# First mixture matrix in 8 KB runs, and the turn of the inner values moved between the scatter or gather products

## The chip, the cores and the metric

One core of one Trainium2 chip runs the whole program. The time is device microseconds (us) of one execution; the number that counts is the median of several. The engines are PE (the matrix engine; its loads of stationary operands are listed as PEld), DVE, ACT, POOL and SP. In this kernel SP issues nearly all of the loads from memory, and the 16 DMA engines of the core move them.

## The reference, cut to what matters

Two layers over 256 tokens of 2048 features, in float32. Each layer has a mixer (retention and convolution in the first, sparse attention in the second), a norm, and then a mixture of 16 experts of which every token takes two:

```
for e in range(N_EXPERTS):
    a, b = jnp.split(xt @ w_gu[e], 2, axis=-1)
    y = y + gate[:, e:e + 1] * ((jax.nn.silu(a) * b) @ w_down[e])
```

`w_gu[e]` is 2048 x 1024 (8 MB) and is here called the first matrix, `w_down[e]` is 512 x 2048 (4 MB), the second. A layer reads 16 x 12 MB for its mixture, whatever the routing is.

## The kernel before, in words

The tokens of an expert are gathered into 64 slots, so that the products of a mixture are small beside the weights that they read. Experts go in pairs `i` = 0..7 with members `j` = 0, 1. The order of the work is written out by hand in `moe` (L1020 to L1048); each engine works through its own list in that order.

- Weights come in chunks of 1 MB, one DMA each, through the list that `plan` makes (L115 to L123). A chunk fills one of 22 pages of 8 KB a partition. `pump` (L145) issues the next chunk from SP as soon as a page is free and fewer than `ringmax` chunks (16 in most of a mixture) are held. A chunk of the first matrix (L118) has 256 rows as 2 blocks of 128: row p of each block lies in partition p, so each partition takes two separate runs of 4 KB. A chunk of the second matrix (L121) is 128 rows of 2048 values: one run of 8 KB a partition, the megabyte as a whole contiguous in memory. The four chunks of the last expert's second matrix are columns, in runs of 2 KB.
- `gather(i, c)` (L865) makes 512 features of the slots of a pair: the tokens `h` are the stationary operand, 128 columns at a time, a one-hot matrix is the moving one. Each product is two loads and two products in the trace. ACT or DVE copies the result to `X[i]`.
- `gu(i, j)` (L894) takes 8 chunks and multiplies 64 slots by them, with two products side by side in the two column halves of the array; then ACT (silu, L907) and DVE (product, L908) make the inner values `sl`.
- `turn` (L911) transposes `sl` on PE (L914) and ACT copies it to `gT` (L916); `down(i, j, gT)` (L931) multiplies `gT` by four chunks of the second matrix, and ACT and DVE (L928, L929) make the rows `Y`.
- `scatter(i)` (L964) puts the rows of a pair at their tokens: 8 blocks of 4 products (L951), each followed by a DVE addition (L959 for the first pair, L961 later).
- For a pair the order is: `gu(i, 0)`, `scatter(i - 1)`, `turn`, `down(i, 0)`, `gather(i + 1, 0 and 1)`, `gu(i, 1)`, `gather(i + 1, 2 and 3)`, `gates(i + 1)` (L877, transposes and products with 2 columns), `turn`, `down(i, 1)`. The PSUM tiles of gather, scatter and turn share 4 banks (L172).
- After the last `gu` come its `turn` (L1044), a branch for experts with too many tokens (L1061), and `last_down` (L972), which uses the last four chunks.

Of the kernel before, what the change touches and what calls it, by code (L numbers as in the profile page):

```python
# [19 lines left out]
P = 128  # L20
# [11 lines left out]
# columns of the constant arrays  # L32
# [48 lines left out]
class Trunk:  # L81
# [9 lines left out]
    # ---------------------------------------------------------------- pages of 8 KB a partition  # L91
# [5 lines left out]
    def drop(self, n=1):  # L97
        """n pages have seen their last use"""
        self.free += n
        self.pump()  # L100

    # ---------------------------------------------------------------- weights
    def plan(self):
        a = self.a
        ch = []

        def dense(w, cols, order):
            for g, kc in order:
                c0, n = cols[g]
                if n == 512:  # L110
                    ch.append((w[kc * 512:(kc + 1) * 512, c0:c0 + n].rearrange("(c p) n -> p c n", p=P), [P, 4, n]))
                else:
                    ch.append((w[:, c0:c0 + n].rearrange("(c p) n -> p c n", p=P), [P, 16, n]))

        def moe(layer):  # L115
            for e in range(NE):
                for k in range(8):
                    ch.append((a["moe_w_gu"][layer, e, k * 256:(k + 1) * 256, :].rearrange("(c p) n -> p c n", p=P), [P, 2, 1024]))  # L118
                for k in range(4):
                    if e < NE - 1:  # L120
                        ch.append((a["moe_w_down"][layer, e, k * P:(k + 1) * P, :].rearrange("(c p) n -> p c n", p=P), [P, 1, 2048]))  # L121
                    else:
                        ch.append((a["moe_w_down"][layer, e, :, k * 512:(k + 1) * 512].rearrange("(c p) n -> p c n", p=P), [P, 4, 512]))  # L123

        # of each projection (column group, part of the rows), in the order of their use
        std = lambda n: [(g, kc) for g in range(n) for kc in range(4)]
        cols = [(c * 512, 512) for c in range(4)]
        self.eorder = [(g, kc) for g in range(4) for kc in (2, 3, 0, 1)]
        self.oorder = [(g, kc) for g in (0, 1) for kc in (0, 1, 2)] + [(0, 3), (1, 3)] + [(g, kc) for g in (2, 3) for kc in range(4)]
        self.ecols = [4096, 5120, 4608, 5632, 0, 512, 1024, 1536, 2048, 2560, 3072, 3584]  # L130
        dense(a["even_w_in"][0], [(c, 512) for c in self.ecols], std(12))
        dense(a["even_w_out"][0], cols, self.eorder)
        moe(0)
        self.ocols = [(3072, 512), (3584, 512), (4096, 80), (2048, 512), (2560, 512)] + [(c * 512, 512) for c in range(4)]
        dense(a["odd_w_in"][0], self.ocols, [(g, kc) for g, kc in std(9) if g != 2 or kc == 0])
        dense(a["odd_w_out"][0], cols, self.oorder)
        moe(1)
        self.chunks = ch
        self.next = 0
        self.got = {}  # L140
        self.use = 0
        self.ring = 0
        self.ringmax = 1
# [27 lines left out]
    # ---------------------------------------------------------------- helpers  # L171
# [34 lines left out]
    # ---------------------------------------------------------------- dense projections  # L206
    def units(self, groups, order=None):
        """the steps of projections: two blocks of rows each (four of a narrow group)"""
        us = []
        seen = {}  # L210
        for i, kc in order or [(i, kc) for i, g in enumerate(groups) for kc in range(4 if g.n == 512 else 1)]:
            g = groups[i]
            for s in range(2 if g.n == 512 else 4):
                n = seen[i] = seen.get(i, -1) + 1
                if g.n == 512:
                    us.append(dict(g=g, k=kc * 4 + s * 2, first=n == 0, last=n == 7, sub=s, nsub=2, w=2))
                else:
                    us.append(dict(g=g, k=s * 4, first=s == 0, last=s == 3, sub=s, nsub=4, w=4))
        return us
# [51 lines left out]
    def dense(self, us, between, hooks=None, budget=1.3, ahead=3, tail=5):  # L271
        hooks = hooks or {}
        n = 0
# [18 lines left out]
        # the end of the last group: one token tile, then the other  # L292
# [10 lines left out]
    # ---------------------------------------------------------------- start  # L303
    def setup(self):
# [20 lines left out]
        # x and the first weights in the pieces and the order of their use  # L325
# [26 lines left out]
    def warm(self, n):  # L352
        """products that nobody wants, to keep the clock of the tensor engine up while it waits"""
        ps = self.psum("warm").rearrange("p (a n) -> p a n", a=4)
        for _ in range(n):
            self.nc.tensor.matmul(ps, self.ones, self.ones[:, None, :].to_broadcast([P, 4, P]), start=True, stop=True)

    def table(self, func):
        """have the activation table of func loaded by the time it is wanted"""
        self.nc.scalar.activation(self.tiny, self.neghalf[:, 0:1], func)  # L360
# [40 lines left out]
    def halves(self, name):  # L401
        """the two parts of a transposed operand, each [128, 8, 256] for half of the rows"""
        return [self.page(f"{name}{i}", [P, 8, S], F32R) for i in range(2)]

    # ---------------------------------------------------------------- even layer
# [235 lines left out]
    def rope(self, out, ps, cos, sin, heads, half):  # L641
        """out, ps: [128, heads*2*half]; the halves of each head apart"""
# [26 lines left out]
    def moments(self, t):  # L669
        """1 / std and - mean / std of token tile t"""  # L670
# [6 lines left out]
    def norm(self, c):  # L677
        """columns of (acc - mean) / std, in place"""
# [8 lines left out]
    def normed(self, t):  # L687
        """token tile t of (acc - mean) / std, in place"""
# [10 lines left out]
    def norms(self, kp):  # L699
        """the columns that the turns up to kp + 1 need"""  # L700
# [3 lines left out]
    def turned(self, kp, out, gc, bc):  # L704
        """out = g * turned + b for the two blocks of kp"""
# [14 lines left out]
    # ---------------------------------------------------------------- mixture of experts  # L720
    def route(self, mp, pl):
        """slots, gates and counts: all [128 tokens, 2 tiles, 16 experts]"""
# [15 lines left out]
        # groups: the largest sum of two, the first of the largest ; experts: how many of the group go before each  # L738
# [44 lines left out]
    def onehot(self, i):  # L783
        """slot one-hots of the experts A, B of pair i, in the order A B A"""
# [8 lines left out]
    def moe_begin(self, layer):  # L793
        """what can be done when the first token tile is normed"""
# [8 lines left out]
    def turned_half(self, layer, t, c):  # L803
        """h = g z + b, 512 columns of token tile t turned"""
# [15 lines left out]
    def moe(self, layer, before_last=None):  # L820
# [14 lines left out]
        def back(t, c):  # L835
            """h as it lies in acc"""
# [28 lines left out]
        def gather(i, c):  # L865
            """features 4c to 4c + 3 of the tokens in the slots of pair i, a slot a column"""
            ps = self.psum("psg")
            for b in range(4):
                k = c * 4 + b
                for t in range(2):  # L870
                    nc.tensor.matmul(ps[:, b * P:(b + 1) * P], h[t][:, k * P:(k + 1) * P], self.PT[i][:, t, 0:P], start=t == 0, stop=t == 1)
# [5 lines left out]
        def gates(i):  # L877
            """one-hots with a slot a row, for the orders A B and B A, and the gates of the slots"""
# [15 lines left out]
        def gu(i, j):  # L894
            ps = self.bank("pgu")
            for c in range(8):
# [3 lines left out]
                wv = w.rearrange("p k (ab h f) -> p k ab h f", ab=2, h=2)  # L900
# [18 lines left out]
        # a product of slots with w_down: of each two blocks of 256 columns one lies in the upper rows, the other in the lower,  # L919
        # and the other way round for the second expert, so that in Y[i][:, o] both experts have rows for the same columns  # L920
        def weigh(i, j, half, po, c0):
            """the upper or lower rows of a product times the gates, in two exact parts"""
# [24 lines left out]
        def placed(i, t, c, ps, begun=False):  # L947
            """the rows of the slots at their tokens, 512 columns of tile t"""
# [15 lines left out]
        def scatter(i):  # L964
            if i == 0:
                self.acc = [self.page(f"z{t}") for t in range(2)]
            for t in range(2):
                for c in range(4):
                    spread(i, t, c)
            self.drop(2)  # L970

        def last_down(gT, early):  # L972
            """the last expert, 512 columns after the other up to the statistics of the norm"""
            begun = {}

            def begin(b, alloc):
                """what acc holds, so that the sum stands in PSUM"""
# [42 lines left out]
        for i in range(8):  # L1020
            if i == 7:
                self.ringmax = 8
            if 0 < i < 7:
                self.onehot(i + 1)
            sl = gu(i, 0)
            if i:
                scatter(i - 1)
# [4 lines left out]
            down(i, 0, turn(sl))  # L1032
# [4 lines left out]
            if i < 7:  # L1037
                gather(i + 1, 2)
                gather(i + 1, 3)
                gates(i + 1)  # L1040
                down(i, 1, turn(sl))
# [9 lines left out]
    def overflow(self, layer, rv, h, wide):  # L1051
        """tokens beyond the slots of an expert: every expert over all tokens, with the gates of those alone"""
# [37 lines left out]
    # ---------------------------------------------------------------- odd layer  # L1090
    def odd(self):
# [142 lines left out]
        def q_done(j):  # L1234
            def f(ac):
# [9 lines left out]
                def task():  # L1245
# [5 lines left out]
                    # one head after the other, a step apart  # L1251
# [86 lines left out]
    # ---------------------------------------------------------------- end  # L1338
# [54 lines left out]
```

## Time and profile before

| what | value |
|---|---|
| time, median of 3 runs (lowest to highest) | 1726.28 us (1724.84 to 1727.17) |
| span of the profiled execution | 1722.4 us (no time outside the span is listed for it; the median is 3.9 us longer) |
| PE busy | 1634.8 us, 95% of the span |
| DVE, ACT, POOL busy | 743.9, 500.6, 345.3 us |
| read from memory | 524.7 MB, 306 GB/s over the span |
| mixtures | products L904 from 407.4 to 850 us (first layer) and to 1675.8 us (second) |
| PE waits for chunks of the first matrix (L904) | 10.8 us over the span, at the ends of the mixtures |

The busy share of PE counts an instruction from its start to its modelled end, and neighbours overlap; so 95% says only that PE is seldom idle. For a single stretch it is better to take starts of instructions and to subtract. In the slice lines each of the 40 places stands for 43 us of the span.

### The profile page before, as it was taken

To read this page: it belongs to the slowest core of one execution; us is meant where nothing else is said; L and a number is where in the kernel's file an instruction comes from. 1 tells how busy PE (TensorE), PEld (TensorE's weight loads), DVE (VectorE), ACT (ScalarE), POOL (GpSimd) and SP (SyncE) were. 2 spreads that over 40 slices of the span, in tenths; PEclk is the share of its full clock that TensorE was granted. 3 is DMA by queue.
4 is the path that set the end of the run, shared out by engine and by line. 5 is a ranking of instruction groups with operands and counts; after the bars stand their busy time and mean duration, and the time that the engine had idled before them with its cause. 6 is when DMAs were issued, how large, how long until landed. Compare 5 with 4: busy or idle time off the path is not lost. (4 is left out here: it accounts for less than half of the span.)

```text
span 1722.4 us, 21361 instructions
## 1 busy us (share of the span) xinstructions
PE 1634.8 (95%) x8551; PEld 1031.0 (60%) x8551; DVE 743.9 (43%) x1348; ACT 500.6 (29%) x780; POOL 345.3 (20%) x218
## 2 busy tenths in 40 slices
PE   9999999999999999999789999999999999999974
PEld 7888887885454445443268788788644544444422
DVE  5799987533222222221264675654412322232125
ACT  5434345433111111111054535553311111111101
POOL 1446564430000000000024553434000000000010
PEclk9999999999999999999989999999999999999996
DMA  9655546859999999999954554366899999999992
GB/s 339 218 189 172 171 150 208 300 201 360 372 410 411 413 413 411 415 412 413 401 187 137 167 186 131 123 221 246 342 370 404 414 412 414 412 413 413 412 406 76
DMA packets 155628, 528.29 MB, mean 307 GB/s; under 512 B 10506, under 2 KB 10898, under 8 KB 140034
## 3 DMA queue, kind: packets, MB, share of 16 engines
q1 hardware_dynamic: 154898, 525.32, 80.2%
q8 instruction: 71, 1.16, 0.3%
q0 software_dynamic: 480, 1.46, 0.2%
q14 instruction: 35, 0.29, 0.0%
q10 hardware_dynamic: 144, 0.07, 0.0%
HBM read 524.71 MB, written 2.10 MB: 306 GB/s over the span
## 5 line engine op out<-in xcount | busy, mean ns | idle before, releaser
L904 PE MATMUL pgu<-w,X 128*64 128x512 f32 x2048 | 450.9, 594 | 11.0 <-DMA w<-in_moe_w_gu_dram 10.8
L236 POOL TENSOR_TENSOR sp<-w,sp 128x1024 fp32r<-128x1024 f32 (+1 forms) x108 | 273.0, 2535 | 402.5 <-ACT sp L233 377.2
L904 PEld LDWEIGHTS pgu<-w,X 128*64 128x64 f32 x2048 | 143.7, 137 | 300.2 <-issue 267.3
L233 ACT ACTIVATE sp<-w 128x1024 fp32r<-128x1024 f32 (+1 forms) x228 | 230.4, 1045 | 121.7 <-PE acc L267 64.1
L236 DVE TENSOR_TENSOR sp<-w,sp 128x1024 fp32r<-128x1024 f32 (+1 forms) x120 | 185.8, 1552 | 130.0 <-ACT sp L233 129.7
L939 PE MATMUL pdn<-w,gT 128*64 128x512 f32 x960 | 212.6, 596 | 16.1 <-ACT gT L916 16.1
L929 DVE SCALAR_TENSOR_TENSOR Yl<-pdn,gs,Yh 64x512 fp32r<-64x512 f32 (+1 forms) x136 | 97.6, 718 | 290.5 <-ACT Yh L928 276.7
L928 ACT ACTIVATE Yh<-pdn,gs 64x512 fp32r<-64x512 f32 (+1 forms) x136 | 89.4, 657 | 283.6 <-PE pdn L939 183.6
L908 DVE TENSOR_TENSOR sl<-sl,pgu 128x256 f32<-128x256 f32 x32 | 13.5, 421 | 354.2 <-ACT sl L907 354.2
L265 PE MATMUL acc<-sp,xhi 128*128 128x512 f32 x384 | 152.4, 397 | 0.0
L939 PEld LDWEIGHTS pdn<-w,gT 128*64 128x64 f32 x960 | 66.3, 137 | 143.1 <-issue 116.1
L266 PE MATMUL acc<-sp,xhi 128*128 128x512 f32 x384 | 149.8, 390 | 0.3 <-DVE sp L236 0.3
L267 PE MATMUL acc<-sp,xlo 128*128 128x512 f32 x384 | 149.9, 390 | 0.0
L791 POOL COPY pt<-pt 128x128 f32<-128x128 f32 x16 | 5.0, 314 | 714.1 <-DVE pt L790 714.1
L907 ACT ACTIVATE sl<-pgu 128x256 f32<-128x256 f32 x32 | 12.3, 384 | 387.1 <-PE pgu L904 377.0
L469 DVE SCALAR_TENSOR_TENSOR pcv<-up,cw,pcv 128x255 f32<-128x255 f32 (+14 forms) x240 | 113.2, 472 | 7.3
L265 PE MATMUL acc<-sp,hhi 128*128 128x512 f32 x256 | 106.1, 414 | 1.2 <-ACT hhi L1116 1.2
L267 PE MATMUL acc<-sp,hlo 128*128 128x512 f32 x256 | 101.1, 395 | 1.2 <-DVE hlo L1117 1.2
L266 PE MATMUL acc<-sp,hhi 128*128 128x512 f32 x256 | 100.6, 393 | 0.0
L266 PEld LDWEIGHTS acc<-sp,xhi 128*128 128x128 f32 x384 | 72.3, 188 | 15.3 <-DVE sp L236 1.0
L267 PEld LDWEIGHTS acc<-sp,xlo 128*128 128x128 f32 x384 | 72.1, 188 | 15.2
L265 PEld LDWEIGHTS acc<-sp,xhi 128*128 128x128 f32 x384 | 72.3, 188 | 14.8 <-ACT sp L233 0.4
(305 smaller groups left out, 2050.7 us busy)
## 6 DMA issues: line engine op xcount, KB each, us to landing
w<-in_moe_w_gu_dram SPq DMA_DIRECT2D x256, 1024.0 KB, 17.6
w<-in_moe_w_down_dram SPq DMA_DIRECT2D x128, 1024.0 KB, 18.4
w<-in_even_w_in_dram SPq DMA_DIRECT2D x46, 1024.0 KB, 5.3
w<-in_odd_w_in_dram SPq DMA_DIRECT2D x32, 1024.0 KB, 5.4
w<-in_even_w_out_dram SPq DMA_DIRECT2D x16, 1024.0 KB, 8.6
w<-in_odd_w_out_dram SPq DMA_DIRECT2D x16, 1024.0 KB, 5.5
acc<-in_x_dram SPq DMA_DIRECT2D x8, 256.0 KB, 8.3
w<-in_even_w_in_dram SPq DMA_DIRECT2D x4, 512.0 KB, 6.7
```

The source lines that it names most:

```text
L233: nc.scalar.activation(sp[:, 0], src, AF.Copy)
L236: eng.tensor_tensor(sp[:, 1], src, sp[:, 0].bitcast(F32), ALU.subtract)
L265: nc.tensor.matmul(ac, xh[:, x], wh, start=st, stop=False)
L266: nc.tensor.matmul(ac, xh[:, x], wl, start=False, stop=False)
L267: nc.tensor.matmul(ac, xl[:, x], wh, start=False, stop=en)
L469: nc.vector.scalar_tensor_tensor(y, up[:, c, 0:S - i], w, y, op0=ALU.mult, op1=ALU.add)
L904: nc.tensor.matmul(ps[h * 64:(h + 1) * 64, :], X[i][:, k, j * 64:(j + 1) * 64], wv[:, kk, :, h, :], start=k == 0, stop=k == KT - 1)
L907: nc.scalar.activation(sl, ps[:, 0:256], AF.Silu)
L908: V.tensor_tensor(sl, sl, ps[:, 256:512], ALU.mult)
L928: nc.scalar.activation(hi, po[r, :], AF.Copy, scale=g)
L929: V.scalar_tensor_tensor(lo, po[r, :], g, hi.bitcast(F32), op0=ALU.mult, op1=ALU.subtract)
L939: nc.tensor.matmul(po[b][half * 64:(half + 1) * 64, :], gT[:, c, h * 64:(h + 1) * 64], wv[:, half ^ j, 2 * b:2 * b + 2, :], start=kk == 0, ...
```

## The change

In `plan` a chunk of the first matrix is read with partition p holding the rows 2p and 2p + 1 of its 256, so each partition takes one run of 8 KB. The k-th block of 128 features of `X` therefore has to hold every second feature of 256; `gather` takes its stationary operand from `h` with a step of two values. `turn` stands after the first token tile of the scatter (j = 0) or between the third and fourth part of the gather (j = 1). For the first member of the first pair, and for the last member of the last pair, its place stays.

```
     def plan / moe(layer):
-        ch.append((a["moe_w_gu"][layer, e, k * 256:(k + 1) * 256, :].rearrange("(c p) n -> p c n", p=P), [P, 2, 1024]))
+        ch.append((a["moe_w_gu"][layer, e, k * 256:(k + 1) * 256, :].rearrange("(p c) n -> p (c n)", c=2), [P, 2048]))
...
     def gather(i, c):
-                k = c * 4 + b
-                for t in range(2):
-                    nc.tensor.matmul(ps[:, b * P:(b + 1) * P], h[t][:, k * P:(k + 1) * P], self.PT[i][:, t, 0:P], start=t == 0, stop=t == 1)
+                q, r = divmod(c * 4 + b, 2)
+                for t in range(2):
+                    f = h[t].rearrange("p (q j r) -> p q r j", q=8, r=2)[:, q, r, :]
+                    nc.tensor.matmul(ps[:, b * P:(b + 1) * P], f, self.PT[i][:, t, 0:P], start=t == 0, stop=t == 1)
...
     def gu(i, j):
-                wv = w.rearrange("p k (ab h f) -> p k ab h f", ab=2, h=2)
+                wv = w.rearrange("p (k ab h f) -> p k ab h f", k=2, ab=2, h=2)
...
-        def scatter(i):
-            if i == 0:
+        def scatter(i, t):
+            if i == 0 and t == 0:
                 self.acc = [self.page(f"z{t}") for t in range(2)]
-            for t in range(2):
-                for c in range(4):
-                    spread(i, t, c)
-            self.drop(2)
+            for c in range(4):
+                spread(i, t, c)
+            if t == 1:
+                self.drop(2)
...
             sl = gu(i, 0)
             if i:
-                scatter(i - 1)
+                scatter(i - 1, 0)
+                gT = turn(sl)
+                scatter(i - 1, 1)
             else:
                 self.onehot(1)
                 gates(0)
                 self.ringmax = 16
-            down(i, 0, turn(sl))
+                gT = turn(sl)
+            down(i, 0, gT)
...
                 gather(i + 1, 2)
+                gT = turn(sl)
                 gather(i + 1, 3)
                 gates(i + 1)
-                down(i, 1, turn(sl))
+                down(i, 1, gT)
```

## Rows read from the trace of the kernel before

**Rows 1.** The page's slices: the busy share of the DMA engines and the bytes moved, 43 us a place.

```profile
DMA  9655546859999999999954554366899999999992
GB/s 339 218 189 172 171 150 208 300 201 360 372 410 411 413 413 411 415 412 413 401 187 137 167 186 131 123 221 246 342 370 404 414 412 414 412 413 413 412 406 76
```

**Rows 2.** Busy time of the engines in stretches of the two mixtures: stretch, length, PE, PEld, DVE, ACT, POOL with counts, granted clock, busy share of the 16 DMA engines, GB/s.

```profile
404.00:444.00 40.00, 39.53 (x232) 20.60 (x232) 7.57 (x18) 5.88 (x10) 0.29 (x1) 1.00 0.86 317
444.00:500.00 56.00, 54.94 (x305) 26.27 (x303) 13.92 (x25) 8.78 (x15) 0.32 (x1) 1.00 1.01 408
...
1270.00:1600.00 330.00, 323.33 (x1782) 154.46 (x1779) 80.52 (x146) 50.67 (x87) 1.93 (x6) 1.00 1.02 412
```

**Rows 3.** PE in order of time at the end of the first layer's mixture: start, length, line, products; in brackets the idle time before and who ended it.

```profile
802.81 8.75 PE L904 MATMUL pgu<-w,X 128*64 128x512 f32 x40
...
819.11 0.39 PE L951 MATMUL psa<-Yh,gtt 128*128 128x256 f32 x1
...
831.00 3.96 PE L904 MATMUL pgu<-w,X 128*64 128x512 f32 x16
835.59 1.94 PE L904 MATMUL pgu<-w,X 128*64 128x512 f32 x8 [0.62 <-DMA w<-in_moe_w_gu_dram]
838.15 1.94 PE L904 MATMUL pgu<-w,X 128*64 128x512 f32 x8 [0.62 <-DMA w<-in_moe_w_gu_dram]
...
848.43 1.94 PE L904 MATMUL pgu<-w,X 128*64 128x512 f32 x8 [0.67 <-DMA w<-in_moe_w_gu_dram]
...
857.91 3.75 PE L980 MATMUL psb<-z,cst 128*128 128x512 f32 x4 [6.16 <-PEq L1061]
```

**Rows 4.** The same view at the end of the second layer's mixture.

```profile
1628.87 8.85 PE L904 MATMUL pgu<-w,X 128*64 128x512 f32 x40
...
1645.16 0.39 PE L951 MATMUL psa<-Yh,gtt 128*128 128x256 f32 x1
...
1657.05 3.60 PE L904 MATMUL pgu<-w,X 128*64 128x512 f32 x16
...
1673.88 1.94 PE L904 MATMUL pgu<-w,X 128*64 128x512 f32 x8 [0.71 <-DMA w<-in_moe_w_gu_dram]
```

**Rows 5.** The same view in the middle of the first layer's mixture, where PE works through a `gu` and a gather without waiting.

```profile
465.20 13.90 PE L904 MATMUL pgu<-w,X 128*64 128x512 f32 x64
479.04 0.38 PE L951 MATMUL psa<-Yh,gtt 128*128 128x256 f32 x1
...
491.03 3.84 PE L871 MATMUL psg<-pt,acc 128*128 128x128 f32 x32
494.80 13.95 PE L904 MATMUL pgu<-w,X 128*64 128x512 f32 x64
```

**Rows 6.** Packets of two stretches: in 551 to 569.6 us only first-matrix chunks move, in 602.3 to 610 us only second-matrix chunks. The 113 and 49 packets under 512 B are the signals at the ends of DMAs.

```profile
DMA packets 1965, 7.60 MB, mean 409 GB/s; under 512 B 113, under 2 KB 113, under 8 KB 1964
...
DMA packets 444, 3.24 MB, mean 420 GB/s; under 512 B 49, under 2 KB 49, under 8 KB 49
```

**Rows 7.** Stretches in which chunks of one matrix alone move, by turns the first (18 us or so) and the second (7 to 8 us); columns as in rows 2.

```profile
520.50:539.30 18.80, 18.80 (x102) 8.67 (x98) 7.20 (x15) 3.12 (x5) 0.32 (x1) 1.00 1.02 409
541.10:549.30 8.20, 8.20 (x48) 3.88 (x44) 1.08 (x2) 1.71 (x3) 0.00 (x0) 1.00 1.01 419
...
571.90:579.60 7.70, 7.70 (x39) 2.59 (x36) 1.03 (x2) 1.67 (x3) 0.00 (x0) 1.00 1.01 421
582.00:600.00 18.00, 17.47 (x96) 8.35 (x94) 6.29 (x14) 0.77 (x2) 0.32 (x1) 1.00 1.03 409
...
612.20:630.40 18.20, 17.67 (x106) 9.09 (x104) 1.27 (x3) 1.96 (x4) 0.00 (x0) 1.00 1.03 410
632.70:640.40 7.70, 7.70 (x38) 2.59 (x36) 3.74 (x8) 2.73 (x4) 0.32 (x1) 1.00 1.01 417
```

**Rows 8.** Packets from 444 to 846 us (first layer) and from 1270 to 1672 us (second).

```profile
DMA packets 36308, 165.51 MB, mean 412 GB/s; under 512 B 2521, under 2 KB 2521, under 8 KB 29629
...
DMA packets 36349, 165.45 MB, mean 412 GB/s; under 512 B 2555, under 2 KB 2587, under 8 KB 29671
```

**Rows 9.** What PE waited for from 444 to 846 us and from 1270 to 1676 us: total, times, longest.

```profile
PE pdn L939 <- ACT gT L916: 7.5, 14, 0.5
...
PE pdn L939 <- ACT gT L916: 7.7, 14, 0.8
```

**Rows 10.** All engines in order of time around a `turn` after a gather.

```profile
456.52 0.95 PE L887 MATMUL pgs<-gate,pt 128*128 128x2 f32 x8
...
457.34 0.42 PE L914 MATMUL pst<-cst,sl 128*128 128x128 f32 x2
...
457.85 0.38 ACT L916 ACTIVATE gT<-pst 128x256 f32<-128x256 f32 x1 [0.53 <-PE pst L914]
```

**Rows 11.** The loads of the gather's stationary operand, one layer: count, shortest, median and longest in ns.

```profile
L871 PEld LDWEIGHTS psg<-pt,acc x512: 185/192/193, 403.6 to 793.5; 128*128 128x128 f32 x171
```

**Rows 12.** DVE at a scatter: the last step of the inner values, then the eight additions.

```profile
479.57 0.42 DVE L908 TENSOR_TENSOR sl<-sl,pgu 128x256 f32<-128x256 f32 x1 [8.99 <-ACT sl L907]
479.91 4.87 DVE L959 SCALAR_TENSOR_TENSOR z<-acc,psa 128x512 f32<-128x512 f32 x8
```

**Rows 13.** What the SP queue waited for before it issued chunks, 405 to 455 us; then the stretch from 496 to 502 us with the columns of rows 2.

```profile
SPq L150 <- PE pgu L904: 43.4, 16, 16.0
...
496.00:502.00 6.00, 6.00 (x30) 2.01 (x28) 0.47 (x1) 0.00 (x0) 0.00 (x0) 1.00 1.02 380
```

## The prediction

> **What bounds the kernel now.** I read the slice lines of the page first [rows 1]. The DMA engines are full in two plateaus of some 400 us each at 401 to 415 GB/s, and these are the mixtures; elsewhere they move far less. A busy PE stands beside them, so the next view is the table of stretches [rows 2]. From 404 to 444 us the DMA engines are at 0.86: SP then waits for PE to give pages back [rows 13]. From 444 us on they stay at 1.01 or 1.02 for the rest of the plateau, and so from 1270 us in the second layer. PE in the same stretches shows short gaps only. Which of the two ends last is seen at the ends of the plateaus, in PE's order of time [rows 3, 4]. There PE does a chunk in 1.94 us and then idles until the next lands; the starts lie 2.56 us apart (835.59, 838.15). PE is the faster of the two: over a mixture it eats up the 16 chunks that lie ready, and then runs at the pace of the DMA. The wait that ends last is the landing of the last chunk of the first matrix; behind it come a turn, a branch (6.16 us) and the last products, which hang on nothing but that.
>
> How far ahead is PE? Without waiting, a `gu` takes 479.04 - 465.20 = 13.84 us to the next product [rows 5]. The first `gu` of the last pair took 819.11 - 802.81 = 16.30 us, 2.46 too many; the second 848.43 + 1.94 - 831.00 = 19.37 against 13.95, 5.42 too many [rows 3, 5]. So PE could have been done 7.9 us earlier in the first layer. In the second it is 16.29 - 13.84 and 18.77 - 13.95, together 7.3 us [rows 4, 5].
>
> **The change part by part.**
>
> *8 KB runs.* The second matrix already comes in the form that the first gets: 1 MB in a piece, one run of 8 KB a partition. The packets show that a run stays one packet: in a stretch of first-matrix chunks all but one are under 8 KB, in a stretch of second-matrix chunks only the signals are [rows 6]. The stretches with one matrix alone give 409, 409, 409 and 410 GB/s for 4 KB and 419, 420, 421 and 417 for 8 KB [rows 6, 7]. A chunk of 1,048,576 bytes takes 2.562 us at 409.25 and 2.501 us at 419.25: 0.061 us less. From 444 to 846 us there are 29,629 - 2,521 = 27,108 packets of 4 KB (256 a chunk), so 105.9 first-matrix chunks; in the second layer 27,084, so 105.8 [rows 8]. 106 x 0.061 = 6.4 us a layer, 12.9 us in all. The rates that lie closest (410, 417) give 0.043 us a chunk, 9.0 us; those furthest apart (409, 421) 0.073 us, 15.4 us. SP issues as many DMAs as before, in the same order, and waits for the same pages; no queue is passed.
>
> Not all of it need arrive. Early in a mixture the DMA is close to running dry because PE has no page to give back: from 496 to 502 us it moved 380 GB/s [rows 13]. What the faster DMA has gained by then (22 chunks since 444 us, two thirds of them the first matrix, 0.9 us) can be lost there. But the pages come from PE, and PE is 1.06 us earlier by then through two turns of the next part. I take the two as cancelling; bounds are -1 and +1 us a layer.
>
> *The turn.* Before, PE waits 0.53 us between the transposes and `down`, for ACT's copy: 7.5 us in 14 waits and 7.7 in 14 [rows 9, 10]. After, four blocks of the scatter (half of 3.9 us) or a gather of 16 products and the gates stand between. The transposes need `sl`: DVE is done with it at 479.99, and half of the scatter ends at about 481.0 [rows 5, 12], so they find it ready. In the banks the turn now takes the fifth place of a ring of four, and waits for the first addition: at 0.61 us each (4.87 / 8) that ends at about 480.5 [rows 12], in time. ACT's queue holds nothing ahead of the copy but a copy of the gather that is ready. Were this cover gone, the 0.53 us would stand as before. So PE saves 7.4 us a layer, but PE is not what ends last: it only waits longer for chunks. Worth 0 for the time, apart from the early pages above.
>
> *The gather with a step of two.* No load of a stationary operand in the trace reads with a step, so this is bounded. Below: nothing, since a packed read is already the densest (no gain). Above: every load twice as long. A load by itself is seen in the gates, whose products have 2 columns: 8 in 457.34 - 456.52 = 0.82 us, 102 ns each [rows 10]. A product of the gather comes every 3.77 / 32 = 118 ns [rows 5], so the load is what paces it, and a longer load shows at once. 512 loads a layer [rows 11] x 102 ns = 52 us. I take 0, the packed rows, as the nearest. PE has room for some: 7.9 - 6.4 + 7.4 = 8.9 us a layer, 17 ns a load, costs nothing. The Trainium skill (SBUF — State Buffer, "Door 1: The DMA port swizzle") says that reads keep full rate as long as two fall into each 16-byte line, and float32 with a step of two does just that; no run here shows it yet. By it the sum stays.
>
> *Sum.* Against the profiled span: 1722.4 - 12.9 = 1709.5 us. The median is 3.9 us above that span, which nothing here touches: 1713.4 us. The end behind the last chunk moves along unchanged, as does the mixer of the second layer. Its clock stays as it is: PE idles before the branch as before.
>
> **The rivals.**
>
> *The gather pays for the step (slower).* One mechanism: loads of `h` at L871 take longer, PE becomes the bound of both mixtures, and the DMA waits for pages. It decides from 17 ns a load; from (7.9 + 7.4) / 512 = 30 ns on, the time is above that of before. At 51 ns (half more) a layer gets 26 - 15 = 11 us longer, 1748 us; at double 37 us, about 1800 us. For it: the load paces the gather. Against it: nothing in the trace either way.
>
> *Only part of the rate comes from the length of the runs.* The second matrix could be quicker for another reason, such as its place. With half of 0.061 us a chunk the gain is 6.4 us: 1720 us. Against it: the stretches alternate every 10 to 20 us and the two rates never meet [rows 6, 7], and the form is the same to the byte. The Trainium skill (DMA: Bandwidth & Descriptors, "Why small descriptors are slow (HBM only)") gives about 3 cycles a packet beside one per 32 bytes. By that two packets of 4 KB cost 2 x 131 cycles and one of 8 KB 259, 1.1% less, an estimate of 0.029 us a chunk, and the time would be 1720 us. The rows show 2.4%, which speaks for more than that rule.
>
> *The change does nothing.* If the 8 KB runs were cut into 4 KB packets, the DMA would keep its pace, the turn would only lengthen PE's waits, and the time would stay at 1726 us. Against it stand the packets of the second matrix [rows 6].
>
> *More than forecast.* If the early pages come sooner as well, a layer gains 1 us more and the rates are those furthest apart: 1726.3 - 15.4 - 2 = 1709 us.
>
> **How the numbers follow.** Forecast as summed (1709 to 1718 us): 0.70. Half of the rate (1718 to 1722 us): 0.08. Nothing: 0.06. Gather slower (over 1730 us): 0.13. Still faster than 1709 us: 0.03. The range of 8 in 10 is 1708 to 1723 us: it leaves out the slow gather and most of the case without effect. Within 0.2% (3.5 us, about what a measurement of this kernel can tell from no change) lies the case without effect: faster 0.81, same 0.06, slower 0.13.
>
> **What would show each step.** In the packets, nearly all of a mixture are 8 KB. The plateaus read about 419 GB/s throughout, and at their ends a chunk of `gu` starts every 2.50 us instead of 2.56. PE's waits for `gT` are gone but for the first pair, and its waits for first-matrix chunks are at least as long as before. L871 keeps 118 ns a product. The forecast is wrong if the gather's 32 products take clearly more than 3.8 us, if the plateaus stay at 412 GB/s, or if PE no longer waits for chunks at the end of a mixture.

## The result, and the profile after

The changed kernel takes 1710.24 us (median of 4 runs, 1705.55 to 1713.20) against 1726.25 us before: ratio 0.9909, 95% interval 0.9891 to 0.9927. Measured twice more beside the experiments it gave 0.9923 (0.9905 to 0.9941) and 0.9904 (0.9884 to 0.9924). So the change saves 0.8 to 1.0%, 12 to 16 us. 1713.4 us were forecast for the median. The sum itself was made for the span of the profiled execution: 1709.5 us, and that span is now 1708.6 us.

The page of the changed kernel: the slices of the DMA engines, bytes moved and packets, as in [rows 1].

```profile
DMA  9655545858999999999954554357899999999992
GB/s 341 216 196 173 172 148 192 304 197 353 376 411 421 421 421 420 422 420 420 407 186 139 171 176 145 124 200 267 319 358 416 422 420 421 421 421 420 421 413 76
DMA packets 122860, 528.29 MB, mean 309 GB/s; under 512 B 10506, under 2 KB 10898, under 8 KB 74498
```

The plateaus stand at 420 to 422 GB/s where they stood at 410 to 415, and are full as before. The kernel before had 155,628 packets, 140,034 of them under 8 KB; 65,536 of those have gone, the 256 chunks with 256 runs of 4 KB each, and half as many of 8 KB have come.

The stretches, columns as in [rows 2]:

```profile
404.00:444.00 40.00, 39.53 (x230) 21.00 (x230) 7.57 (x18) 5.88 (x10) 0.29 (x1) 1.00 0.82 305
444.00:500.00 56.00, 56.00 (x310) 27.08 (x308) 13.91 (x25) 8.68 (x15) 0.33 (x1) 1.00 1.01 415
500.00:800.00 300.00, 300.00 (x1646) 145.51 (x1644) 71.60 (x129) 46.30 (x81) 1.62 (x5) 1.00 1.01 420
```

From 404 to 444 us, where the DMA waits for pages, a quicker DMA only idles more (0.82 where it was 0.86). From 444 us on it is full, and there the gain is made. The gaps that PE had at the turns have gone: it is busy 300.00 of 300 us from 500 to 800 us.

PE in order of time at the end of the first layer's mixture, as [rows 3]:

```profile
798.79 14.01 PE L907 MATMUL pgu<-w,X 128*64 128x512 f32 x64
...
824.19 3.61 PE L907 MATMUL pgu<-w,X 128*64 128x512 f32 x16
828.34 1.94 PE L907 MATMUL pgu<-w,X 128*64 128x512 f32 x8 [0.55 <-DMA w<-in_moe_w_gu_dram]
830.83 1.94 PE L907 MATMUL pgu<-w,X 128*64 128x512 f32 x8 [0.56 <-DMA w<-in_moe_w_gu_dram]
...
840.82 1.94 PE L907 MATMUL pgu<-w,X 128*64 128x512 f32 x8 [0.58 <-DMA w<-in_moe_w_gu_dram]
...
850.32 3.75 PE L983 MATMUL psb<-z,cst 128*128 128x512 f32 x4 [6.19 <-PEq L1070]
```

The reader is to see the same end as before, 7.6 us earlier (850.32 against 857.91): PE still waits for each chunk, which now comes every 2.49 us instead of 2.56. The first `gu` of the last pair runs without a wait, though; PE is ahead by the second alone, 840.82 + 1.94 - 824.19 - 13.95 = 4.6 us. In the second layer both `gu` of the last pair still wait:

```profile
1617.75 10.47 PE L907 MATMUL pgu<-w,X 128*64 128x512 f32 x48
...
1632.64 0.39 PE L954 MATMUL psa<-Yh,gtt 128*128 128x256 f32 x1
...
1644.10 3.60 PE L907 MATMUL pgu<-w,X 128*64 128x512 f32 x16
...
1660.75 1.94 PE L907 MATMUL pgu<-w,X 128*64 128x512 f32 x8 [0.65 <-DMA w<-in_moe_w_gu_dram]
```

1632.64 - 1617.75 - 13.84 and 1660.75 + 1.94 - 1644.10 - 13.95 make 5.7 us together. And the turn, between two halves of a gather at the end of the second layer:

```profile
1605.42 2.15 PE L874 MATMUL psg<-pt,z 128*128 128x128 f32 x16
1607.41 0.38 PE L917 MATMUL pst<-cst,sl 128*128 128x128 f32 x2
1607.63 2.05 PE L874 MATMUL psg<-pt,z 128*128 128x128 f32 x16
```

Nothing stands idle around it, where PE waited 0.53 us before [rows 9]. The 16 products of a gather take 1607.41 - 1605.42 = 1.99 us, 124 ns each.

### The profile page after: what moved, and what is told of

Its sections match the earlier page's. It is cut to its first block, busy times and chain, and to the rows that moved or that the text cites. A ratio compares the mean times of both kernels' runs of the same rounds, so it can differ in the third digit from the quotient of the medians.

```text
span 1708.6 us, 21350 instructions
## 1 busy us (share of the span) xinstructions
PE 1639.9 (96%) x8551; PEld 1039.2 (61%) x8551; DVE 743.3 (44%) x1348; ACT 499.5 (29%) x780; POOL 345.4 (20%) x218
## 3 DMA queue, kind: packets, MB, share of 16 engines
q8 instruction: 71, 1.16, 0.3%
```

## The experiments

Each diff is against the changed kernel. "Mixture" is the time from the first to the last load of `gu`, first and second layer, in the profiled execution; it is free of what the clock does elsewhere. The three profiles of the changed kernel lie within 0.6 us of each other in it. Times of a row are compared with the kernel before on the same chip.

| kernel | time, us | ratio to before (95%) | mixtures, us |
|---|---|---|---|
| before | 1724 to 1726 | | 442.0, 441.6 |
| changed | 1710.2 | 0.9909 (0.9891 to 0.9927) | 434.1, 435.1 |
| changed, again | 1712.1 | 0.9923 (0.9905 to 0.9941) | 434.7, 434.7 |
| changed, third time | 1708.5 | 0.9904 (0.9884 to 0.9924) | 434.7, 434.6 |
| e1 old place of the turn | 1713.9 | 0.9940 (0.9923 to 0.9957) | 437.1, 437.2 |
| e2 turn alone | 1721.8 | 0.9990 (0.9977 to 1.0003) | 441.2, 441.0 |
| e3 packed gather, old place | 1712.3 | 0.9933 (0.9916 to 0.9950) | 435.7, 434.5 |
| e4 same rows in 4 KB runs | 1724.8 | 1.0003 (0.9991 to 1.0015) | 441.6, 441.4 |
| e5 second matrix in 4 KB runs | 1717.7 | 0.9959 (0.9945 to 0.9974) | 439.7, 438.1 |
| e6 step of 4 | 1813.2 | 1.0515 (1.0496 to 1.0534) | 484.8, 484.8 |
| e7 step of 16, one run | 1802.0 | | 477.7, 477.6 |
| e8 gather behind `gu` | 1706.9 | 0.9904 (0.9883 to 0.9925) | 433.3, 433.0 |

**The changed kernel again.**

> The changed kernel once more, beside the others on one chip. Theory A (the DMA's rate is the gain): 1710 us, a spread of some 4 us. A second question is the spread of the first four times (1705.6 to 1713.2 us): if it belongs to the kernel, it comes again and goes with the granted clock of the run; if it was that chip, the times lie within 2 us.

1712.08 us, from 1707.24 to 1713.05: two runs at 1707 with a granted clock of 0.986, four at 1711.5 to 1713 with 0.980 to 0.982. So the spread, 5.8 us where some 4 were expected, comes again with the program and goes with the clock; more on it at the end.

**e1, the runs without the turn.** Both calls of `turn` go back to where they stood; runs and gather stay changed.

```
                 scatter(i - 1, 0)
-                gT = turn(sl)
                 scatter(i - 1, 1)
+                gT = turn(sl)
...
                 gather(i + 1, 2)
-                gT = turn(sl)
                 gather(i + 1, 3)
                 gates(i + 1)
+                gT = turn(sl)
```

> 8 KB runs and the gather with a step of two, the turn where it was. Theory A': the DMA gains 6.7 us a layer, but the stepped gather costs PE 6 ns a load (124 instead of 118 ns a product, 3.2 us a layer), and without the turn's 7.4 us PE has only 7.9 - 3.2 = 4.7 us of room in the first layer and 4.1 in the second: PE becomes the bound by 2 to 3 us a layer, 1717 us, and waits for chunks almost nowhere. Theory A in its plain form (the turn is worth nothing for the time): 1710 us. Rival B (the turn is the gain): 1726 us.

1713.89 us, between the plain form and the expected 1717. In the trace PE is the bound: between 444 and 850 us this kernel's list of PE's waits holds its 14 turns, the last turn of the layer and no wait for a chunk.

```profile
PE pdn L942 <- ACT gT L919: 7.5, 14, 0.5
PE pst L917 <- DVE sl L911: 0.9, 1, 0.9
```

Its mixtures are 3.0 and 2.1 us longer than those of the first profile of the changed kernel, as Theory A' said (2 to 3 us a layer). In times that is less clear: 1.8 us more than the changed kernel beside it, whose own runs spread over 6 us.

**e2, the turn without the runs.** The chunk, the view in `gu` and the gather are those of before.

```
-                    ch.append((a["moe_w_gu"][layer, e, k * 256:(k + 1) * 256, :].rearrange("(p c) n -> p (c n)", c=2), [P, 2048]))
+                    ch.append((a["moe_w_gu"][layer, e, k * 256:(k + 1) * 256, :].rearrange("(c p) n -> p c n", p=P), [P, 2, 1024]))
...
-                    f = h[t].rearrange("p (q j r) -> p q r j", q=8, r=2)[:, q, r, :]
+                    f = h[t][:, (c * 4 + b) * P:(c * 4 + b + 1) * P]
...
```

> 4 KB runs and the packed gather as before, the turn in its new place. Theory A: 1726 us, within 1.5 us of before; the last matmuls wait about 7 us a layer longer for chunks. Rival B: 1711 us.

1721.78 us, ratio 0.9990, with 1 in its interval. The median is 2.7 us below that of before, more than the 1.5 that were allowed; by the mixtures the turn alone is worth 0.6 to 0.8 us a layer, hardly more than two profiles of one kernel differ. PE's saving turns into waiting. The waits for chunks from 444 to 850 us, in this kernel and then in the kernel before:

```profile
PE pgu L907 <- DMA w<-in_moe_w_gu_dram: 10.2, 17, 0.7
```

```profile
PE pgu L904 <- DMA w<-in_moe_w_gu_dram: 5.6, 9, 0.7
```

The list holds 4.6 us more, where about 7 were expected; the 7.5 us of the turns [rows 9] have gone from it. It leaves out short gaps. By the starts of its products, as in the prediction, the last four `gu` of this layer take 2.8, 1.2, 4.5 and 6.0 us too many, 14.5 us where the last two took 7.9 too many before: 6.6 us more, so the expectation holds. Rival B falls.

**e3, the runs with the old turn and a packed gather.** As e1, and `f` as in e2; the gather then brings other features than those that the chunk's rows belong to.

> 8 KB runs, the turn where it was, and the gather reading 128 neighbouring values (features and rows of the first matrix then do not belong together; the work is the same in kind and amount). Theory A': PE has 7.9 - 6.7 = 1.2 us of room a layer, so the DMA's gain comes whole: 1711 us, and the difference to the run with the stepped gather (5 to 6 us) is the price of the step where nothing hides it. If the step is free: the same time in both.

1712.30 us, mixtures 435.7 and 434.5: the DMA's gain is there without the turn, when the step costs nothing. Against e1 the mixtures are 1.4 and 2.7 us shorter. In the second layer this kernel waits for no chunk from 1256 us on, so 2.7 us is about the whole price of the step; in the first its last `gu` waits for two chunks and is 1.6 us too long, so that part of the price stays hidden there. The times differ by 1.6 us, not by the 5 to 6 that I wrote; they show little of the 4.1 us of the mixtures, since the runs of e1 had a granted clock of 0.983 to 0.986 and those of this kernel 0.981 to 0.984.

**e4, the same rows in 4 KB runs.**

```
-                self.nc.sync.dma_start(t, src)
+                for o in range(2):
+                    self.nc.sync.dma_start(t[:, o * 1024:(o + 1) * 1024], src[:, o * 1024:(o + 1) * 1024])
```

This holds for chunks of the first matrix only.

> The changed kernel, but each chunk of the first matrix comes by two DMAs of 512 KB: the same rows in the same partitions, in runs of 4 KB instead of 8. Theory A (the length of a run sets the rate): 409 GB/s and 2.56 us a chunk again, 1724 us, PE waiting for chunks some 10 us a layer as with the turn alone. Rival C (the order of the rows or the place in memory sets it): 420 GB/s and 1711 us.

1724.79 us, ratio 1.0003: the whole gain has gone. Stretches of this kernel with the first, the second, the first and the second matrix alone:

```profile
521.60:539.80 18.20, 18.20 (x100) 8.64 (x98) 7.65 (x16) 2.81 (x5) 0.32 (x1) 1.00 1.02 409
542.30:549.70 7.40, 7.40 (x47) 4.33 (x44) 2.22 (x3) 2.05 (x3) 0.00 (x0) 1.00 1.00 415
582.40:600.60 18.20, 18.20 (x100) 8.56 (x98) 5.21 (x9) 0.77 (x2) 0.00 (x0) 1.00 1.03 409
603.00:610.60 7.60, 7.60 (x49) 4.58 (x49) 2.96 (x5) 2.64 (x4) 0.00 (x0) 1.00 1.02 421
```

409 GB/s for the first matrix again, with the rows in the new order. (It also has twice the DMAs for this matrix; that they cost nothing by themselves is seen in that 409 is the rate of before.) This is the run that differs from the changed kernel in the runs alone: its mixtures are 6.3 to 7.5 us longer than those of the three profiles of the changed kernel. PE's list from 444 to 850 us holds 5.5 us of waits for chunks in 27 pieces, not the 10 that were expected; each chunk now lands in two halves, and no piece is longer than 0.3 us.

**e5, the second matrix in 4 KB runs.** The same two lines for the chunks of the second matrix, not those of a layer's last expert.

> The changed kernel, but each chunk of the second matrix (not those of a layer's last expert) comes by two DMAs of 4 KB runs. Theory A: first-matrix chunks stay at 2.49 us, second-matrix chunks go from 2.49 to 2.56: 52 x 0.07 = 3.6 us a layer, 7 us in all, 1718 us. Rival C (the second matrix is quick by itself): no change, 1711 us.

1717.67 us, 1718 expected. The first matrix and the second in turn:

```profile
523.10:540.10 17.00, 17.00 (x91) 7.74 (x88) 6.45 (x14) 2.81 (x5) 0.32 (x1) 1.00 1.01 422
542.80:550.30 7.50, 7.50 (x44) 3.88 (x41) 1.50 (x2) 2.05 (x3) 0.00 (x0) 1.00 1.02 407
584.90:600.50 15.60, 15.60 (x88) 7.83 (x86) 5.21 (x9) 0.77 (x2) 0.00 (x0) 1.00 1.01 420
604.50:610.70 6.20, 6.20 (x42) 3.98 (x42) 2.95 (x4) 2.52 (x4) 0.00 (x0) 1.00 1.02 408
```

The two matrices have changed places: 422 and 420 for the first, 407 and 408 for the second. In e4 and e5 the rate goes with the length of the run, whichever matrix it is and in whichever order its rows lie. Rival C falls.

**e6 and e7, longer steps in the gather.** 16 blocks of 128 features are taken with a step of 4 (or 16) values; features and rows do not belong together then.

```
-                q, r = divmod(c * 4 + b, 2)
+                q, r = divmod(c * 4 + b, 4)
...
-                    f = h[t].rearrange("p (q j r) -> p q r j", q=8, r=2)[:, q, r, :]
+                    f = h[t].rearrange("p (q j r) -> p q r j", q=4, r=4)[:, q, r, :]
```

> The changed kernel with the gather's stationary operand read with a step of 4 values (16 bytes) instead of 2 (features and rows then do not belong together; the work is the same in kind and amount). The rival of the prediction, that the gather pays for its step, made larger. Theory A: PE has 4.6 us of room a layer, 9 ns a load. If a load takes twice as long (102 ns more): 52 us a layer, less the room 47, about 1805 us, and PE waits for no chunk. If it costs another 6 ns as the step of 2 did: 3 us a layer, within the room, 1711 us.

> The same with a step of 16 values (64 bytes). If a load pays for each 16-byte line that it touches, step 4 and step 16 cost the same (one value a line in both). If it pays by distance, this one is dearer: over twice the price of step 4.

1813.24 us and 1802.01 us. The loads of the gather's stationary operand in the changed kernel, with a step of 4, and with 16 (count, shortest, median, longest in ns), each from its own trace:

```profile
L874 PEld LDWEIGHTS psg<-pt,acc x512: 193/197/197, 403.6 to 790.3; 128*128 128x128 f32 x171
```

```profile
L874 PEld LDWEIGHTS psg<-pt,acc x512: 308/330/332, 405.3 to 851.0; 128*128 128x128 f32 x171
```

```profile
L874 PEld LDWEIGHTS psg<-pt,acc x512: 291/311/316, 405.5 to 844.6; 128*128 128x128 f32 x171
```

Packed it was 192 ns [rows 11]; a step of 2 makes it 197, of 4 330, of 16 311. So step 2 falls in one class with the packed read, and steps 4 and 16 in another: the price comes where only one value is left in 16 bytes, and it does not grow with the distance. That step 16 is 19 ns cheaper than step 4, where the same was expected, stays open, and no other step was run. PE at a gather with a step of 4, and the `gu` behind it:

```profile
507.23 7.73 PE L874 MATMUL psg<-pt,acc 128*128 128x128 f32 x32
514.89 13.95 PE L907 MATMUL pgu<-w,X 128*64 128x512 f32 x64
```

(514.89 - 507.23) / 32 = 239 ns a product, 118 packed: 121 ns more, where the doubled load of the expectation (102 ns more) gave about 1805 us. From 410 to 900 us PE waits for no chunk. The DMA, full before, now waits for pages: from 500 to 800 us it moves

```profile
500.00:800.00 300.00, 300.00 (x1441) 164.25 (x1441) 64.24 (x114) 42.16 (x73) 1.29 (x4) 1.00 0.96 392
```

392 GB/s at a share of 0.96. This is the slow rival of the prediction, with its mechanism in place; with a step of 2 it does not come, with a step of 4 it does.

**e8, pages given back earlier.** For pairs 1 and 2 the first two parts of the gather stand behind the `gu` that they preceded.

```
-            if i < 7:
+            if 1 < i < 7:
                 gather(i + 1, 0)
                 gather(i + 1, 1)
             sl = gu(i, 1)
+            if i < 2:
+                gather(i + 1, 0)
+                gather(i + 1, 1)
```

> The changed kernel, with the first two parts of the gather for pairs 1 and 2 behind the second gu of the pair before instead of ahead of it, so that PE gives pages back 4 us earlier where the DMA runs dry at the start of a mixture (idle gaps at 433, 441 and 497 us). Theory A: the last dry point sets the rest of the mixture; the DMA restarts up to 1.5 us earlier a layer, 2 to 3 us in all, 1708 us beside 1711 us; the stretch from 404 to 444 us moves more than 305 GB/s. If later gaps take it back: no change.

> The changed kernel beside it, on the same chip: 1711 us, in two clusters some 5 us apart as before.

1706.93 us beside 1708.49; the intervals of the ratios overlap, so the times alone don't show it. The mixtures are 1.4 and 1.6 us shorter, 3.0 us in all, as Theory A said. In the stretches of this kernel the DMA moves more at first and less behind:

```profile
404.00:444.00 40.00, 39.53 (x216) 18.63 (x217) 6.93 (x17) 5.29 (x9) 0.29 (x1) 1.00 0.86 334
444.00:500.00 56.00, 56.00 (x310) 27.20 (x308) 13.91 (x25) 8.68 (x15) 0.32 (x1) 1.00 0.99 407
```

334 against 305 GB/s in the kernel beside it, then 407 against 414. In bytes that is 13.35 against 12.19 MB, then 22.81 against 23.20, and 125.84 against 126.03 from 500 to 800 us: 1.16 MB won and 0.58 lost again, so half of what is won by 444 us goes into later gaps. The other half, at 420 GB/s, is the 1.4 us.

## Why the prediction was right

**The runs.** "106 x 0.061 = 6.4 us a layer": the mixtures became 7.9 and 6.5 us shorter in the first profile after, 7.3 and 6.9 in the second, 7.3 and 7.0 in the third. Against e4, which has 4 KB runs and the rest of the change, it is 6.3 to 7.5 us. The mechanism is shown by e4 and e5, from both sides. The term was some 10% small: chunks come 0.07 us sooner (2.49 for 2.56), and 106 x 0.07 = 7.4. The rates of short stretches, read to whole GB/s, gave 0.061; the starts of PE's waiting products would have given 2.56 at once, and no row of before gave 2.49 as sharply.

**The pages.** "Bounds are -1 and +1 us a layer" held: a quicker DMA did idle more before 444 us, and what the mixtures gained (6.5 to 7.9 us) lies between 0.9 us under and 0.5 us over the 7.4 of the rate. That early pages and early idling cancel was not shown apart.

**The step.** "I take 0": it is 6 ns a product, 3.1 us a layer over 512 products, and not visible in the time since PE had room. So the sign "L871 keeps 118 ns a product" failed, if by little (124 ns). The cause is confirmed by e6 and e7. The Trainium skill (SBUF — State Buffer, "Door 1: The DMA port swizzle") states two accesses a 16-byte line as enough. The trace agrees but for a small rest: with two the load is 5 ns longer, with one 119 to 138 ns.

**The turn.** "Worth 0 for the time" was right for a turn by itself (e2, 0.6 to 0.8 us a layer) and wrong beside the other parts. Here the step of the prediction that failed is the room: "8.9 us a layer". Measured are 4.6 us in the first layer and 5.7 in the second, and the sign that PE waits for first-matrix chunks "at least as long as before" failed with it: 3.3 us in 6 waits where 5.6 us in 9 stood. Of its terms the turn's 7.4 us was right. In e2, where the gather is packed, a scatter and a gather with their turns take

```profile
479.61 0.39 PE L954 MATMUL psa<-Yh,gtt 128*128 128x256 f32 x1
...
484.16 2.37 PE L942 MATMUL pdn<-w,gT 128*64 128x512 f32 x10
```

```profile
453.65 2.05 PE L874 MATMUL psg<-pt,acc 128*128 128x128 f32 x16
...
458.86 7.09 PE L942 MATMUL pdn<-w,gT 128*64 128x512 f32 x32
```

484.16 - 479.61 = 4.55 us and 458.86 - 453.65 = 5.21 us to the start of `down`; before it was

```profile
484.01 1.51 PE L939 MATMUL pdn<-w,gT 128*64 128x512 f32 x6 [0.53 <-ACT gT L916]
```

```profile
452.41 3.84 PE L871 MATMUL psg<-pt,acc 128*128 128x128 f32 x32
...
458.29 7.09 PE L939 MATMUL pdn<-w,gT 128*64 128x512 f32 x32 [0.53 <-ACT gT L916]
```

484.01 - 479.04 = 4.97 us [rows 5] and 458.29 - 452.41 = 5.88 us. That is 1.09 us a pair, 7.6 us a layer. (One thing was missed on the way: in the second half of a scatter two starts lie 0.27 us apart, where 0.12 us is the rule,

```profile
481.84 0.28 PE L954 MATMUL psa<-Yl,gtt 128*128 128x256 f32 x1
482.11 0.38 PE L954 MATMUL psa<-Yh,gtt 128*128 128x256 f32 x1
```

and so they do in e2, but not in e1, where the turn has its old place. So this wait comes with the turn's new place, and the 7.6 us hold with it.) The DMA's gain was put in too small and the step of the gather at nothing. In the first profile after, the mixtures gained 7.9 and 6.5 us where 6.4 was put in, and the step takes 2.9 us of a mixture (32 of the 512 products lie ahead of it): 7.9 - 7.9 + 7.6 - 2.9 = 4.7 us, and 7.3 - 6.5 + 7.6 - 2.9 = 5.5 us in the second layer, so that nothing of size is left over. Without the turn's saving the room would be below zero, and e1 shows it so: PE waits for no chunk, and the mixtures are 2 to 3 us longer. The turn thus pays for the step.

**The sum.** The span was forecast to 0.9 us, and that is in part luck: the mixtures gained 14.4 us in this profile and 14.2 and 14.3 in its repetitions, where 12.9 was put in, and 0.6 us of it went outside the mixtures, where profiles of one kernel differ by more than that. The median was forecast 3.2 us too high, and 2.3 us of that are the term "3.9 us above that span, which nothing here touches": after the change the median is 1.6 us above the profiled span. In the runs that list both, 1.7 to 2.0 us lie outside the span; the rest of the 3.9 us is probably the execution that the profile had fallen on.

**The rivals.** "Only part of the rate" falls by e4 and e5. The estimate from the Trainium skill (DMA: Bandwidth & Descriptors, "Why small descriptors are slow (HBM only)") was 1.1%. Measured are 2.7% (2.56 to 2.49), so half as many packets save more here than that page's 3 cycles a packet account for; what else they save was not measured. "Does nothing" falls by the packet counts. "The gather pays" falls for a step of two and comes true in e6 for a step of four.

## What to carry to other kernels

Where two engines run nearly level, find which ends last from the end of the stretch, not from busy shares: a transfer that has 2.7% to gain is worth that on every byte moved while it is the bound, and nothing where it waits for pages. An edit that is "free" on the other engine uses up its room; add up all such edits against the measured room before calling any of them worth nothing. Reading a float32 stationary operand of 128 columns with a step of two cost 6 ns a product here; with a step of four the products came every 239 ns instead of 118.

## What was not expected

The times of one kernel spread with the granted clock: the changed kernel took 1705 to 1708.5 us with 0.985 to 0.988 and 1709 to 1713 us with 0.980 to 0.983, and the kernel before from 1718 to 1729 us in the same way. One such place can be seen, in the mixer of the first layer. The stretches of the profile after (the second line is for the end of the mixture), and then of its repetition:

```profile
276.00:284.00 8.00, 6.37 (x36) 5.47 (x37) 3.02 (x4) 5.51 (x11) 0.51 (x1) 1.00 0.06 5
...
845.80:856.00 10.20, 5.68 (x14) 2.41 (x16) 0.00 (x0) 0.00 (x0) 0.00 (x0) 0.50 1.05 384
```

```profile
276.00:284.00 8.00, 6.60 (x29) 5.75 (x30) 3.02 (x4) 5.74 (x12) 0.28 (x1) 0.79 0.00 0
```

PE does the same work around a pause there; in one execution the granted clock stayed at 1.00, in the other part of the stretch was granted 1.2 GHz, and the mixture began 1.5 us later (409.1 against 407.6). The other profiles fall in the same two groups: leaving out the two with long steps, the mixture begins at 407.3 to 408.3 us in the six that have 1.00 from 276 to 284 us, and at 408.6 to 409.1 us in the four that have 0.79.

The other place is behind the last chunk of each mixture, where PE idles 6 us at the branch and the clock is at its lower level (0.50 in the second line of the profile after). No profile of the changed kernel fell on an execution of 1705 us, but that of e8 did (1704.64 us, 0.986), and there the clock was back sooner, behind a mixture that ended 0.7 us earlier:

```profile
845.80:856.00 10.20, 6.41 (x32) 3.10 (x33) 0.37 (x1) 0.47 (x1) 0.00 (x0) 0.67 1.05 383
```

How much of the 5 us comes from there stays open. For a change of 0.1% the length of a stretch in the trace told more than the medians.
